# Keys and queries of a third head ahead of the second layer's norm, and one convolution ahead of the fourth head's projections

## The chip, the cores and the metric

The kernel runs on one NeuronCore of a Trainium2 chip. The metric is the device time of one execution in microseconds (us), given as the median of three runs of the kernel before.

## The reference

Two groups of tokens, 128 context tokens and 256 latent tokens, go through two layers with the same weights. Each layer norms and modulates its input `x`, projects it once to everything that three mixers need, projects their joined outputs back onto `x`, and then runs a squared-ReLU MLP.

```python
h = _rmsnorm(xs, norm_mix[d]) * (1.0 + ca) + sa
q, k, v, gb, gc, xin, u, vs = _project(h, w_in[d])
...
att = _diff_attention(q, k_all, v_all, lam, subln[d], lam_init)
conv = gb * _short_conv(gc * xin, conv_w[d], conv_b[d])
cmlp = _chunk_mlp(u, vs, w_s[d], b_s[d])
xs = xs + ga * (jnp.concatenate([att, conv, cmlp], axis=-1) @ w_out[d])
h = _rmsnorm(xs, norm_mlp[d]) * (1.0 + cm) + sm
xs = xs + gm * _mlp(h, w_up[d], w_down[d])
```

The attention has four heads; each takes the difference of two softmaxes. Context tokens attend to themselves, latent tokens to a cache and to themselves. All of it is in float32.

## The kernel before

**Precision and tiles.** Every long product is made of three matmuls in a faster 32-bit format: high part times high part (L220), high part of the weight times low part of the input (L221), low part of the weight times high part of the input (L222). `hh` and `hl` are the two parts of the input, 8 tiles of 128 features by 384 tokens. A weight chunk of 128x1024 arrives by DMA as `raw`; ScalarE (ACT) rounds it into `whi` (L201) and VectorE (DVE) makes `wlo` of the rest (L203).

**Order of the work.** The order on PE (TensorE), ACT, DVE and POOL (GpSimd) is written out by hand. The long products advance a clock by one tick per contraction step (three matmuls). All other work is cut into stages by Python generators, and a stage's number in the table `WAIT` says how many ticks go by before the next stage is issued. Ticks only set the order of the instructions on each engine; at run time an engine waits for what the next instruction of its list needs.

**The second layer's mixer.** While the last MLP tile of the first layer ends, `hh` and `hl` hold `x` times its feature scale, without the token's norm and without the shift. The keys and queries of the first `NPRE[d]` heads are projected from this form (tiles `pkq`, L634, 386 columns of which two carry the shift), and DVE multiplies the norm in when it moves them out of PSUM (`evict_all`, L512 and L514). Then `normed` (L355 to L378) writes the full normed input over `hh` and `hl`, a feature tile per stage: DVE makes `t` (L361), ACT writes `hh` (L369), DVE writes `hl` (L372). It can write a feature tile only when the last `pkq` product has read it, and `wait_normed` says at which tick it starts. PE goes on with the values (`nat`, `proj_tokens`, L448 to L450; two feature tiles to a weight chunk, three groups of tokens to a feature tile), which read each feature tile of the full norm, then with the later heads' keys and queries (`later_heads`), two convolutions (`conv`) and the chunk MLP.

**Attention.** Each head has three units `u` of 128 queries (`attention`, L720): scores `sc` (two PSUM tiles, L728 for the context unit, L731 and L732 for the others), their maxima on DVE (`nm`, L736), exponentials on ACT (`e`, L741), a scaling on DVE and ACT (L745 to L749), a transposition on PE (`pt`, L753), and after the third unit the product with the values (`po`). Units of a head are 8 ticks apart (`unit`), heads 24 (`head`), and the first starts `unit0` ticks after the values begin. The tiles `sc` and `pt` take turns in three PSUM buffers of the tag `misc`:

```python
def misc_tile(name="misc"):
    return ps.tile([P, 512], F32, tag="misc", name=name, bufs=3)
...
    for u in range(3):
        go(attention(h, u))
        yield wt["unit"]
```

Rotary positions (`rope_apply`) use a shuffle on DVE (L648) and three operations on POOL; `keys` and `queries` then make their parts on ACT (L666, L669, L682) and DVE (L670, L685).

Of the kernel before, what the change touches and what calls it, by code (L numbers as in the profile page):

```python
# [27 lines left out]
# heads of a layer whose products go ahead of the norm  # L28
NPRE = (3, 2)
# parts of the first modulation vector  # L30
PARTS = 4

# contraction steps between the stages of the work beside the long products, by layer
# [29 lines left out]
    "fh0": (14, 14),  # L63
# [9 lines left out]
    "wait_normed": (1, 12),  # L73
# [6 lines left out]
    "unit0": (24, 24),  # L80
    "head": (24, 24),
    "late": (0, 5),
# [4 lines left out]
# columns of the packed small operands: those of all layers that come first, then the rest  # L87
# [5 lines left out]
# order of the 128-column tiles of the input projection  # L93
Q0, K0, V0, GB0, GC0, XI0, U0, VS0 = 0, 512, 1024, 1536, 1792, 2048, 2304, 2560

# tokens, followed by one column for the shift of each group
# [4 lines left out]
def dit_kernel(ctx, tc, xT, cT, wmod, wmodT, wall, ck, cv, ws, lam, bs_in, small, rope, ident_in, yT, kT_out, v_out):  # L101
    nc = tc.nc
# [9 lines left out]
    # ---- constants and inputs  # L112
# [16 lines left out]
    # silu of the two conditioning vectors, as padded stationary columns  # L129
# [8 lines left out]
    # ---- the order of work: every engine runs in the order below. What is not part of the long  # L138
    # products is cut into stages; a stage names how many contraction steps of the long products
    # go by before the next one.  # L140
# [33 lines left out]
    def steps(gen, n, every):  # L174
        """n stages of a generator"""
        for i in range(n):
            next(gen, None)
            if i < n - 1:
                yield every

    # ---- weight streaming
# [8 lines left out]
    def refill(r=None):  # L190
        """the next chunk of the weights, in two parts"""
        i = state["chunk"]
        if i == wall.shape[0]:
            return
        state["chunk"] = i + 1
        if r is None:
            r = raw_chunk(wall[i])
        hi = wpool.tile([P, 1024], F32R, tag="whi", name="whi", bufs=4)
        lo = wpool.tile([P, 1024], F32R, tag="wlo", name="wlo", bufs=4)
        ready.append((hi, lo))  # L200
        nc.scalar.copy(hi, r)  # L201
        yield 2
        nc.vector.tensor_sub(lo, r, hi.bitcast(F32))  # L203
# [13 lines left out]
    def mm3(out, w, a, wsl, asl, first, last):  # L217
        """out += w.T @ a from the parts of both, w stationary"""
        (wh, wl), (ah, al) = w, a
        mm(out, wh[wsl], ah[asl], start=first, stop=False)  # L220
        mm(out, wh[wsl], al[asl], start=False, stop=False)  # L221
        mm(out, wl[wsl], ah[asl], start=False, stop=last)  # L222

    # ---- modulation vectors, features on partitions: modv[d][:, v, dt, group]
# [4 lines left out]
    def mod_done(d, v, base, dts=slice(0, KT)):  # L229
        """modv[d][:, v] = base + b_mod, and what scales the normed input"""  # L230

        def column(o):
            c = sm[:, d * S_LAYER + o + dts.start : d * S_LAYER + o + dts.stop]
            return c.unsqueeze(2).to_broadcast([P, dts.stop - dts.start, 2])

        nc.vector.tensor_add(modv[d][:, v, dts], base[:, dts], column(S_BMOD + v * KT))
        if v in (1, 4):
            nc.vector.scalar_tensor_tensor(
                (amix if v == 1 else amlp)[d][:, dts],
                modv[d][:, v, dts],  # L240
                1.0,
                column(S_NMIX if v == 1 else S_NMLP),
                ALU.add,
                ALU.mult,
            )

    def mod_products():
        """on the tensor engine: one feature tile of the contraction per step"""
        for i, (d, v) in enumerate(MOD_PE):
            pm = ps.tile([P, 256], F32, tag="mod", name="pm", bufs=1)  # L250
            tr = work.tile([P, KT, 32], F32, name="tr", tag="rtmp", bufs=1)
            # the first vector comes in parts of its features
            n = per = PARTS if i == 0 else 1
            width = 256 // n
            for f in range(n):
                own = slice(f * width, f * width + width)
                for q in range(KT // per):
                    w = ahead if (i, f, q) == (0, 0, 0) else raw_chunk(wmod[i, f * KT // per + q])
                    for k in range(per):
                        kt = q * per + k  # L260
                        for j in range(4):
                            mm(  # L262
                                pm[32 * j : 32 * j + 32, own],
                                sct[:, kt, :],
                                w[:, (4 * k + j) * width : (4 * k + j + 1) * width],
                                start=(kt == 0),
                                stop=(kt == KT - 1),
                            )
                    yield
                dts = slice(f * KT // n, (f + 1) * KT // n)  # L270
                nc.vector.transpose(tr[:, dts].rearrange("p a b -> p (a b)"), pm[:, own])
                mod_done(d, v, tr[:, :, 0:2], dts)
                yield
# [4 lines left out]
    # the two silu vectors along the free dimension, on every partition  # L278
# [4 lines left out]
    def spread_silu():  # L283
        """their high and low parts as rows, 32 features of each tile a row; then the sums of both parts"""
# [21 lines left out]
    def mod_sums():  # L306
        """on the vector engine: one group of one tile of the vector's features per step"""
        for i, (d, v) in enumerate(MOD_DVE):
            mr = work.tile([P, KT, 2], F32, name="mr", bufs=2)
            for dt in range(KT):  # L310
                w = raw_chunk(wmodT[i, dt])
# [12 lines left out]
    # ---- RMS statistics over the features (partitions)  # L324
# [13 lines left out]
    def rsqrt_refined(y, a, ms):  # L338
        """y ~ ms^-0.5 made exact by one Newton step"""
        nc.vector.tensor_mul(a, y, y)  # L340
        nc.vector.scalar_tensor_tensor(a, a, -0.5, ms, ALU.mult, ALU.mult)
        nc.vector.scalar_tensor_tensor(y, a, 1.5, y, ALU.add, ALU.mult)
# [12 lines left out]
    def normed(scale, shift, every):  # L355
        """the normed and modulated input, a feature tile per stage"""
# [23 lines left out]
    def scaled_high(dt, scale):  # L380
        """a feature tile without its tokens' norms, which products take on afterwards"""
# [24 lines left out]
    def finish_x(dt, pacc, gate, scale, last=False):  # L406
        """the residual stream's tile after a product, and what the next norm needs of it"""
# [12 lines left out]
    def proj_tiles(a, n=1, cols=T, name="acc", order=tuple(range(KT)), later=0, make=acc_tile):  # L420
        """128-column tiles of a weight, transposed: [column, token]"""
# [11 lines left out]
    def proj_tokens(a, width):  # L433
        """`width` columns of a weight, tokens on partitions: three tiles [token, column]"""
# [21 lines left out]
    def shift_products(raws, bias, t0, t1):  # L456
        """what the shift adds to the columns of the raw tiles: [column, tile, group]"""
# [17 lines left out]
    # padded conv input: 0 | prompt | 0 | sample | 0  # L475
# [8 lines left out]
    def lambdas(d):  # L484
# [10 lines left out]
        # -(e1 - e2 + li)  # L495
# [5 lines left out]
    for d in range(DEPTH):  # L501
# [5 lines left out]
        def evict(i):  # L507
            """a head's keys or queries but for the shift's part, which comes later"""
# [20 lines left out]
        # ------------------------------------------------ mixer  # L529
        # products with the tiles of two heads go ahead of the norm  # L530
# [85 lines left out]
        else:  # L616
# [16 lines left out]
            for i in (2, 3):  # L633
                pre.append(proj_tiles(a, 1, TE, "pkq", later=wt["later"]))  # L634
                evict_all(i)
# [17 lines left out]
        def keys(h):  # L653
            """positions, and the parts of the keys by component: the high ones on both halves, the low
            ones next to the queries' high ones"""
# [16 lines left out]
        def queries(h):  # L672
            """positions, and the parts of the sample's queries by component: high and low ones on the
            two halves, the high ones on the component's own"""
# [45 lines left out]
        def attention(h, u):  # L720
            """softmaxes of 128 queries of a head, combined and applied to the values"""
# [56 lines left out]
            # norm of the head's output, tokens on partitions  # L778
# [45 lines left out]
        def conv(ct):  # L824
            """short convolution, channels on partitions"""
# [54 lines left out]
        if d == 0:  # L880
            conv(0)
        later_heads()
        for ct in range(1 - d, 2):
            conv(ct)
# [6 lines left out]
        # output projection  # L891
# [7 lines left out]
        # ------------------------------------------------ MLP  # L899
        if d == 1:  # L900
            start(steps(sums, 2 * KT, wt["sums_up"]), 2)
        for f in range(2):
# [33 lines left out]
            def down(pt, w, c, cols):  # L936
                """half of the contraction of a tile"""
# [13 lines left out]
    # ---- the last tiles, a group of tokens after the other, and the final norm of each group  # L951
# [40 lines left out]
# the vectors (layer, which) in the order of their use, by the engine that makes them  # L992
# [6 lines left out]
def _tiles(w, cols):  # L999
    """[1024, cols of one 128-tile] -> [128, 8 * 128]"""  # L1000
# [5 lines left out]
def _pack(inp):  # L1006
# [6 lines left out]
    # [d, k, (v dt j c)] -> [v, kt, p, (j dt c)] and [v, dt, p, k]  # L1013
    # the first vector: [part, some kt, p, (kt j dt c)]
# [9 lines left out]
    for d in range(DEPTH):  # L1024
# [6 lines left out]
        if d == 0:  # L1031
            chunks += convs[0] + kq[n:] + convs[1]
        else:
            chunks += kq[n:] + convs[0] + convs[1]
# [32 lines left out]
    # axial rotary tables by shape: partition = (component, axis, half, frequency)  # L1067
# [34 lines left out]
```

## Time and profile before

| | us |
|---|---|
| median of three runs (918.04 to 920.19) | 919.28 |
| span of the profiled execution, from its first to its last instruction | 916.9 |
| median less that span (start and end around it) | 2.4 |
| PE busy in the span | 894.1 |
| DVE busy | 652.9 |
| ACT busy | 478.5 |

The page gives no time of its own for the profiled execution, only the span, so its own time is taken as the span and the 2.4 us around it. The second layer's mixer lies at 476 to 600 us of the span. A row of the timeline gives the start, the length, the engine, the line and what is written from what; matmuls overlap, so the distance of two starts is what one costs.

### The profile page before, as it was taken

How to read it: one execution, taken by the hardware profiler on the slowest of the kernel's cores; microseconds unless marked ns; L12 is line 12 of the kernel's file. 1: busy time of each engine (PE TensorE's matmuls, PEld its weight loads, DVE VectorE, ACT ScalarE, POOL GpSimd, SP SyncE). 2: the span in 40 equal slices, each digit the busy share in tenths (PEclk: the TensorE clock that was granted, in tenths of full speed). 3: DMA queues.
4: the chain of work that ended last, by engine and by line, in shares of the span. 5: the costliest groups of instructions: out<-in, count | busy, mean ns of one | idle time of the engine just before them, and what ended most of it. 6: DMA issues, size and time to landing. Idle time of an engine off the chain costs nothing.

```text
span 916.9 us, 14490 instructions
## 1 busy us (share of the span) xinstructions
PE 894.1 (98%) x5476; PEld 839.8 (92%) x5476; DVE 652.9 (71%) x1214; ACT 478.5 (52%) x938; POOL 81.3 (9%) x79
## 2 busy tenths in 40 slices
PE   5999999999999999999999999999999999999996
PEld 4766787999999999999998788999999999999996
DVE  4688886789888877879979877458886344555333
ACT  4557765446762226663336786534676223665331
POOL 0004320011000000000112340003000000000021
PEclk9999999999999999999999899999999999999998
DMA  9877566455656765566773323224465434333302
GB/s 346 298 274 252 192 209 226 165 182 161 209 188 226 227 214 180 183 198 226 221 234 101 125 76 95 91 93 138 163 221 169 137 117 136 115 133 121 115 1 69
DMA packets 48470, 156.55 MB, mean 171 GB/s; under 512 B 5392, under 2 KB 11024, under 8 KB 48400
## 3 DMA queue, kind: packets, MB, share of 16 engines
q1 hardware_dynamic: 48400, 155.63, 51.4%
q8 instruction: 43, 0.70, 0.3%
q14 instruction: 27, 0.22, 0.1%
HBM read 152.98 MB, written 2.62 MB: 170 GB/s over the span
## 4 chain that ended last, share of the span: by engine, by line
PE 91%; DVE 5%; DMA 1%; issue 1%; ACT 1%; POOL 1%; SPq 0%; DVEq 0%; ACTq 0%
PE pdn L220 10%; PE pdn L222 10%; PE pdn L221 10%; PE pup L221 9%; PE pup L220 9%; PE pup L222 9%; PE po L220 2%; PE po L221 2%; PE po L222 2%; PE pm L262 2%; PE pkq L220 2%; PE pkq L221 2%; PE pkq L222 1%; PE po L776 1%; PE nat L448 1%; PE sc L732 1%
## 5 line engine op out<-in xcount | busy, mean ns | idle before, releaser
L201 ACT CAST whi<-raw 128x1024 fp32r<-128x1024 f32 x182 | 190.0, 1050 | 293.3 <-PE pdn L221 150.9
L203 DVE TENSOR_TENSOR wlo<-raw,whi 128x1024 fp32r<-128x1024 f32 x182 | 224.6, 1240 | 64.9 <-ACT whi L201 64.8
L220 PE MATMUL pdn<-ah,whi 128*128 128x384 f32 (+2 forms) x528 | 174.7, 331 | 0.0
L221 PE MATMUL pdn<-al,whi 128*128 128x384 f32 (+2 forms) x528 | 174.6, 331 | 0.0
L222 PE MATMUL pdn<-ah,wlo 128*128 128x384 f32 (+2 forms) x528 | 174.6, 331 | 0.0
L220 PE MATMUL pup<-hh,whi 128*128 128x386 f32 x512 | 174.1, 340 | 0.0
L221 PE MATMUL pup<-hl,whi 128*128 128x386 f32 x512 | 173.6, 339 | 0.3
L222 PE MATMUL pup<-hh,wlo 128*128 128x386 f32 x512 | 172.8, 337 | 0.0
L314 DVE SCALAR_TENSOR_TENSOR junk<-raw,cb 128x1024 bf16<-128x1024 f32 x112 | 136.7, 1220 | 0.4
L221 PEld LDWEIGHTS pdn<-al,whi 128*128 128x128 f32 x528 | 99.2, 188 | 0.0
L220 PEld LDWEIGHTS pdn<-ah,whi 128*128 128x128 f32 x528 | 99.2, 188 | 0.0
L222 PEld LDWEIGHTS pdn<-ah,wlo 128*128 128x128 f32 x528 | 99.2, 188 | 0.0
L221 PEld LDWEIGHTS pup<-hl,whi 128*128 128x128 f32 x512 | 96.9, 189 | 1.1 <-DVE hl L387 0.9
L220 PEld LDWEIGHTS pup<-hh,whi 128*128 128x128 f32 x512 | 96.4, 188 | 0.3
L222 PEld LDWEIGHTS pup<-hh,wlo 128*128 128x128 f32 x512 | 96.5, 188 | 0.0
L336 POOL TENSOR_TENSOR sacc<-sacc,sq 128x384 f32<-128x384 f32 x23 | 29.4, 1279 | 675.6 <-ACT sq L329 533.7
L917 ACT ACTIVATE relu<-relu,ub 128x128 f32<-128x128 f32 (+1 forms) x128 | 51.1, 446 | 17.4 <-DVE relu L914 17.4
L398 DVE SCALAR_TENSOR_TENSOR x<-pdn,modv,x 128x128 f32<-128x128 f32 (+1 forms) x62 | 23.0, 413 | 43.9 <-PE pdn L222 43.9
L921 DVE TENSOR_TENSOR al<-relu,ah 128x384 fp32r<-128x384 f32 x64 | 35.6, 556 | 15.0 <-ACT ah L919 14.8
L220 PE MATMUL po<-y,whi 128*128 128x384 f32 x128 | 43.0, 336 | 0.0
L222 PE MATMUL po<-y,wlo 128*128 128x384 f32 x128 | 42.8, 334 | 0.0
L221 PE MATMUL po<-y,whi 128*128 128x384 f32 x128 | 42.8, 334 | 0.0
(198 smaller groups left out, 1414.1 us busy)
## 6 DMA issues: line engine op xcount, KB each, us to landing
raw<-in_wall_dram SPq DMA_DIRECT2D x182, 512.0 KB, 3.6
raw<-in_wmodT_dram SPq DMA_DIRECT2D x56, 512.0 KB, 4.3
raw<-in_wmod_dram SPq DMA_DIRECT2D x40, 512.0 KB, 5.7
raws<-in_wall_dram SPq DMA_DIRECT2D x6, 512.0 KB, 8.0
x<-in_xT_dram SPq DMA_DIRECT2D x8, 192.0 KB, 7.8
out_dram<-x SPq DMA_DIRECT2D x4, 256.0 KB, 2.6
mix<-in_cv_dram SPq DMA_DIRECT2D x2, 256.0 KB, 5.7
mix<-in_ws_dram SPq DMA_DIRECT2D x2, 256.0 KB, 6.0
```

The costliest lines, as they stand in the source:

```text
L201: nc.scalar.copy(hi, r)
L203: nc.vector.tensor_sub(lo, r, hi.bitcast(F32))
L220: mm(out, wh[wsl], ah[asl], start=first, stop=False)
L221: mm(out, wh[wsl], al[asl], start=False, stop=False)
L222: mm(out, wl[wsl], ah[asl], start=False, stop=last)
L262: mm(pm[32 * j : 32 * j + 32, own], sct[:, kt, :], w[:, (4 * k + j) * width : (4 * k + j + 1) * width], start=(kt == 0), stop=(kt == KT - 1),)
L314: nc.vector.scalar_tensor_tensor(junk, w, 1.0, cb[:, g], ALU.mult, ALU.mult, accum_out=mr[:, dt, g : g + 1])
L336: eng.tensor_add(stat["acc"], stat["acc"], sq)
L398: nc.vector.scalar_tensor_tensor(x[:, dt, a:b], pacc[:, a:b], gate[:, dt, g : g + 1], x[:, dt, a:b], ALU.mult, ALU.add)
L448: mm(o, ah, wh[:, cols], start=(kt == 0 and tt % n == 0), stop=False)
L917: nc.scalar.activation(r[:, s0:s1], r[:, s0:s1], AF.Relu, bias=ub[:, g : g + 1])
L921: nc.vector.tensor_sub(al[:, i], r, ah[:, i].bitcast(F32))
```

## The change

In the second layer the keys and queries of three heads, not two, are projected ahead of the norm; the norm starts 16 ticks later (`wait_normed` 28 for 12), so that it stands to the values as before. The first convolution comes ahead of the later head's keys and queries in both layers (it did so in the first layer already), and the weights are packed in that order. The third head's keys and queries are taken up 16 ticks after the second's, not 14 (`fh0`, which in the second layer had no use before). The first attention unit starts 17 ticks after the values begin, not 24 (`unit0`), and the last two heads have no further delay (`late`). The scratch space for DMA descriptors is made smaller. Comments are taken out, which shifts line numbers from L881 on.

```diff
-NPRE = (3, 2)
+NPRE = (3, 3)
...
-    "fh0": (14, 14),
+    "fh0": (14, 16),
...
-    "wait_normed": (1, 12),
+    "wait_normed": (1, 28),
...
-    "unit0": (24, 24),
+    "unit0": (24, 17),
...
-    "late": (0, 5),
+    "late": (0, 0),
...
-            for i in (2, 3):
+            for i in range(2, 2 * NPRE[d]):
...
-        if d == 0:
-            conv(0)
+        conv(0)
         later_heads()
-        for ct in range(1 - d, 2):
-            conv(ct)
+        conv(1)
...
-        if d == 0:
-            chunks += convs[0] + kq[n:] + convs[1]
-        else:
-            chunks += kq[n:] + convs[0] + convs[1]
+        chunks += convs[0] + kq[n:] + convs[1]
...
-    nc = bacc.Bacc("TRN2", target_bir_lowering=False, num_devices=1)
+    nc = bacc.Bacc("TRN2", target_bir_lowering=False, num_devices=1, dynamic_dma_scratch_size=4096)
```

How this moves instructions is shown at three places, before and after. The number behind a name tells tiles of one name apart; the names in brackets are the engines that a row waits for.

**PE, values of the second layer, the first unit's scores (L728).** Before, they stand behind the sixth of eight feature tiles (`whi_5045` holds the fifth and sixth, `whi_5113` the last two):

```order
L448 MATMUL nat_5084<-whi_5045,hh_97 128x512
L449 MATMUL nat_5084<-wlo_5046,hh_97 128x512
L450 MATMUL nat_5084<-whi_5045,hl_98 128x512
L728 MATMUL sc_5250<-mix_4917 128x128
L728 MATMUL sc_5251<-mix_4917 128x128
L448 MATMUL nat_5082<-whi_5113,hh_97 128x512 [waits Activation_49]
L449 MATMUL nat_5082<-wlo_5114,hh_97 128x512
```

With the change:

```order
L448 MATMUL nat_5149<-whi_5112,hh_97 128x512 [waits Activation_49]
L449 MATMUL nat_5149<-wlo_5113,hh_97 128x512
L450 MATMUL nat_5149<-whi_5112,hl_98 128x512 [waits DVE_49]
L728 MATMUL sc_5280<-mix_4917 128x128
L728 MATMUL sc_5281<-mix_4917 128x128
L448 MATMUL nat_5150<-whi_5112,hh_97 128x512 [waits Activation_49]
L449 MATMUL nat_5150<-wlo_5113,hh_97 128x512
L450 MATMUL nat_5150<-whi_5112,hl_98 128x512 [waits DVE_49]
```

The two score products now stand behind the first token group of the fifth feature tile (`whi_5112` holds the fifth and sixth), five groups earlier.

**PE, the second unit's scores (L731 and L732).** Before, they stand behind the last feature tile of the values, ahead of the third head's keys `pk`:

```order
L448 MATMUL nat_5084<-whi_5113,hh_97 128x512
L449 MATMUL nat_5084<-wlo_5114,hh_97 128x512
L450 MATMUL nat_5084<-whi_5113,hl_98 128x512
L731 MATMUL sc_5294<-kh_5135,qs_5195 128x384
L732 MATMUL sc_5294<-kl_5136,qs_5195 128x384
L731 MATMUL sc_5295<-kh_5135,qs_5195 128x384 [waits Activation_49]
L732 MATMUL sc_5295<-kl_5136,qs_5195 128x384
L220 MATMUL pk_5310<-hh_97,whi_5141 128x384 [waits PE_49]
L221 MATMUL pk_5310<-hl_98,whi_5141 128x384
L222 MATMUL pk_5310<-hh_97,wlo_5142 128x384
```

With the change:

```order
L448 MATMUL nat_5149<-whi_5180,hh_97 128x512 [waits Activation_49]
L449 MATMUL nat_5149<-wlo_5181,hh_97 128x512
L450 MATMUL nat_5149<-whi_5180,hl_98 128x512 [waits DVE_49]
L731 MATMUL sc_5340<-kh_5202,qs_5262 128x384 [waits DVE_49]
L732 MATMUL sc_5340<-kl_5203,qs_5262 128x384
L731 MATMUL sc_5341<-kh_5202,qs_5262 128x384 [waits Activation_49]
L732 MATMUL sc_5341<-kl_5203,qs_5262 128x384
L448 MATMUL nat_5150<-whi_5180,hh_97 128x512
L449 MATMUL nat_5150<-wlo_5181,hh_97 128x512
L450 MATMUL nat_5150<-whi_5180,hl_98 128x512
```

They now stand behind the first token group of the seventh feature tile (`whi_5180` holds the last two), so five groups of the values are queued behind them. The wait of the second product (`sc_5341`) for ACT is there before and after: its PSUM buffer is the one in which the first unit's first scores were.

**DVE, end of the norm (`hl`, L372) and first unit.** Before:

```order
L685 TENSOR_TENSOR qs_5195<-mix_4917,qs_5195 64x256 x2
L372 SCALAR_TENSOR_TENSOR hl_98<-t_5200,modv1_92,hh_97 128x128 [waits Activation_49]
L372 SCALAR_TENSOR_TENSOR hl_98<-t_5200,modv1_92,hh_97 128x256 [waits Activation_49]
L203 TENSOR_TENSOR wlo_5208<-raw_5205,whi_5207 128x1024 [waits DMAHW5_49,PE_49]
L648 STREAM_SHUFFLE rt_5235<-mix_4917 128x256 [waits Pool_49]
L670 TENSOR_TENSOR kl_5229<-mix_4917,kh_5228 64x384 [waits DMAHW4_49,Activation_49]
L670 TENSOR_TENSOR kl_5229<-mix_4917,kh_5228 64x384 [waits Activation_49]
L736 TENSOR_REDUCE nm_5262<-sc_5250 128x1 [waits PE_49]
L736 TENSOR_REDUCE nm_5262<-sc_5251 128x1 [waits PE_49]
L203 TENSOR_TENSOR wlo_5257<-raw_5254,whi_5256 128x1024 [waits DMAHW7_49,Activation_49]
L745 RECIPROCAL s_5270<-s_5270 128x2 [waits Activation_49]
L746 TENSOR_SCALAR s_5270<-s_5270,neg_lam_104 128x1 [waits DVE_49]
```

With the change:

```order
L685 TENSOR_TENSOR qs_5262<-mix_4917,qs_5262 64x256 x2
L372 SCALAR_TENSOR_TENSOR hl_98<-t_5267,modv1_92,hh_97 128x128 [waits Activation_49]
L372 SCALAR_TENSOR_TENSOR hl_98<-t_5267,modv1_92,hh_97 128x256 [waits Activation_49]
L203 TENSOR_TENSOR wlo_5275<-raw_5272,whi_5274 128x1024 [waits DMAHW0_49,PE_49]
L736 TENSOR_REDUCE nm_5296<-sc_5280 128x1 [waits PE_49]
L736 TENSOR_REDUCE nm_5296<-sc_5281 128x1 [waits PE_49]
L648 STREAM_SHUFFLE rt_5313<-mix_4917 128x256 [waits Pool_49]
L670 TENSOR_TENSOR kl_5303<-mix_4917,kh_5302 64x384 [waits DMAHW4_49,Activation_49]
L670 TENSOR_TENSOR kl_5303<-mix_4917,kh_5302 64x384 [waits Activation_49]
L745 RECIPROCAL s_5307<-s_5307 128x2 [waits Activation_49]
L746 TENSOR_SCALAR s_5307<-s_5307,neg_lam_104 128x1 [waits DVE_49]
L749 SCALAR_TENSOR_TENSOR e_5306<-e_5306,s_5307 128x128 [waits Activation_49]
```

The maxima `nm` of the first unit now come ahead of the second head's shuffle and `kl`, and its reciprocal ahead of the next `wlo`. The 44 rows on DVE from the first `t` of the norm (L361) to the `wlo` shown here are the same rows in the same order before and after, and they stand behind the move of the last but one `pkq` tile out of PSUM in both.

## Rows read from the trace of the kernel before

**Rows 1.** the page: its span, and section 1, busy us and share of the span

```profile
span 916.9 us, 14490 instructions
...
PE 894.1 (98%) x5476; PEld 839.8 (92%) x5476; DVE 652.9 (71%) x1214; ACT 478.5 (52%) x938; POOL 81.3 (9%) x79
```

**Rows 2.** windows, 504 to 514 us: length, busy us by engine, PEclk, DMA share, GB/s

```profile
504.00:506.00 2.00, 0.21 (x1) 0.21 (x2) 2.00 (x5) 1.01 (x4) 0.93 (x1) 0.77 0.32 59
506.00:508.00 2.00, 2.00 (x5) 1.61 (x6) 2.00 (x6) 2.00 (x6) 1.34 (x2) 0.50 0.51 207
...
510.00:512.00 2.00, 2.00 (x5) 1.59 (x6) 1.97 (x4) 1.38 (x2) 0.00 (x0) 0.53 0.01 4
512.00:514.00 2.00, 2.00 (x10) 1.64 (x9) 1.94 (x6) 0.00 (x0) 1.38 (x2) 1.00 0.40 115
```

**Rows 3.** the waits of PE, 440 to 640 us: in total, times, longest

```profile
PE nat L450 <- DVE hl L372: 2.8, 1, 2.8
```

**Rows 4.** timeline of PE, 487 to 523 us: start, us, engine, line, operation

```profile
487.50 0.34 PE L220 MATMUL pkq<-hh,whi 128*128 128x386 f32 x1
...
491.73 0.40 PE L448 MATMUL nat<-whi,hh 128*128 128x512 f32 x1
...
492.43 0.39 PE L448 MATMUL nat<-whi,hh 128*128 128x512 f32 x1
...
505.79 0.80 PE L450 MATMUL nat<-whi,hl 128*128 128x512 f32 x1 [2.83 <-DVE hl L372]
506.38 0.63 PE L448 MATMUL nat<-whi,hh 128*128 128x512 f32 x1
...
507.66 0.63 PE L448 MATMUL nat<-whi,hh 128*128 128x512 f32 x1
...
509.07 0.80 PE L728 MATMUL sc<-mix 64*128 64x128 f32 x4
...
515.02 0.34 PE L731 MATMUL sc<-kh,qs 128*128 128x384 f32 x1
...
516.40 0.44 PE L220 MATMUL pk<-hh,whi 128*128 128x384 f32 x1
...
522.21 0.44 PE L220 MATMUL pq<-hh,whi 128*128 128x384 f32 x1
```

**Rows 5.** timeline of DVE, 487 to 518 us

```profile
487.70 0.16 DVE L622 COPY bias<-pkq 128x2 f32<-128x2 f32 x1 [0.98 <-PE pkq L222]
...
505.39 0.73 DVE L372 SCALAR_TENSOR_TENSOR hl<-t,modv,hh 128x128 fp32r<-128x128 f32 x2
...
509.32 0.85 DVE L685 TENSOR_TENSOR qs<-mix,qs 64x256 fp32r<-64x256 f32 x2
...
510.87 1.22 DVE L203 TENSOR_TENSOR wlo<-raw,whi 128x1024 fp32r<-128x1024 f32 x1
...
512.35 1.56 DVE L670 TENSOR_TENSOR kl<-mix,kh 64x384 fp32r<-64x384 f32 x2
513.94 0.49 DVE L736 TENSOR_REDUCE nm<-sc 128x1 f32<-128x128 f32 x2
...
515.60 0.16 DVE L745 RECIPROCAL s<-s 128x2 f32<-128x2 f32 x1
...
516.95 0.35 DVE L749 SCALAR_TENSOR_TENSOR e<-e,s 128x128 f32<-128x128 f32 x1
517.22 1.01 DVE L736 TENSOR_REDUCE nm<-sc 128x1 f32<-128x384 f32 x2
```

**Rows 6.** timeline of ACT, 514 to 519 us

```profile
514.27 0.37 ACT L741 ACTIVATE e<-sc,nm 128x128 f32<-128x128 f32 x1 [2.86 <-DVE nm L736]
...
516.10 0.40 ACT L747 ACTIVATE e<-e,s 128x128 f32<-128x128 f32 x1 [0.31 <-DVE s L746]
...
518.78 0.60 ACT L741 ACTIVATE e<-sc,nm 128x384 f32<-128x384 f32 x1
```

**Rows 7.** the waits of PE weight loads, 60 to 200 us (first layer)

```profile
PEld sc L731 <- ACT e L741: 0.5, 1, 0.5
```

## Prediction

> **What bounds the kernel now.** I read the page first: PE is busy for 98% of the 916.9 us [rows 1], so time can only come from the places where PE waits, or be lost where it begins to. Next I asked for PE's waits from the end of the first layer to the start of the second MLP, the stretch that the change touches: there is one, 2.8 us in the values, for the low part `hl` of a feature tile [rows 3]. It shows again in PE's timeline, idle up to 505.79 [rows 4]. Then the windows around it: the granted clock falls to 0.50 while PE stands (0.77 is the mean of the window in which it falls), and is back at 1.00 only from 512 us [rows 2]. A group of three value matmuls costs 492.43 - 491.73 = 0.70 us at the upper level (2.4 GHz) and 507.66 - 506.38 = 1.28 at the lower (1.2 GHz) [rows 4]. Last the timelines of DVE and ACT: DVE works without a gap from 487.70, when it moves the last but one `pkq` tile out of PSUM, until the `hl` at 505.39 that frees PE and beyond [rows 5]. So PE waits for the amount of work on DVE, not for one slow operation. The median of the runs is 2.4 us above the profiled span; I make the sum as a difference against that execution and put it on the median of 919.28.
>
> **The change, on the old time axis.** A `pkq` tile is 491.73 - 487.50 = 4.23 us [rows 4]. Two more of them come ahead of the values and two fewer behind, so everything from the norm on is 8.46 us later and this is given back after the convolution; the 386 columns instead of 384 are 0.04 us for both tiles, nothing. I leave the 8.46 out of all times below.
>
> *The norm.* DVE's 44 rows from the first `t` to the `wlo` behind the last `hl` are unchanged, and before them stands the same move of a `pkq` tile, which waits for PE (0.98 us idle in front of it [rows 5]), now for the fifth tile instead of the third. So DVE starts the row of work at the same distance to the values and hands over `hl` at the same 505.79. The two tiles that DVE now also moves out fall into the time in which it idles; without that cover they would cost their own length, as the 0.98 us show at most. The wait stays.
>
> *First unit's scores.* They move ahead of that wait. At 509.07 they took up to 0.8 us at the lower level [rows 4]; now I take half, 0.4, at the upper. PE thus arrives 0.4 later and waits 2.4 instead of 2.83; what is saved is the 0.8 that no longer lies behind 505.79.
>
> *Second unit's scores.* PE resumes at 505.79, still at the lower level: the rest of a group, 0.59, then three groups of 1.28, and it stands at the second unit at 510.2. Their input `qs` is done at 509.32 + 0.85 = 510.17 [rows 5], just in time. The first product pair ends at about 511.2 (an estimate: 0.69 for half a unit at the upper level, from 515.02 to 516.40, stretched as the groups are, is 1.26; I take 1.0, since part of it is loading weights). The second pair needs the PSUM buffer of the first unit's scores, hence its exponential. On DVE the maxima come behind the `wlo` that ends at 510.87 + 1.22 = 512.09; before, the exponential began 514.27 - 513.94 = 0.33 after them, and takes 0.37 [rows 5, 6]. So it ends at 512.8, and PE goes on at 512.9: a new wait of 1.7 us. Behind it on PE stand five groups of the values, which everything later waits for. That this buffer can hold PE up is seen in the first layer, where a score's weight load stood 0.5 us for the same exponential [rows 7].
>
> *From there to the third unit.* At the upper level: the pair 0.69, three groups 2.1, and PE asks for the first unit's transposition at 515.7. DVE has it ready at: maxima until 512.58, shuffle and `kl` until about 514.5 (`kl` 1.56), then reciprocal to scaled result 516.95 + 0.35 - 515.60 = 1.70 less the `qs` 0.87 that stood in between (0.85 and its gap), plus 0.4 for waiting on ACT's 0.40: 515.8 [rows 5, 6]. That is even, 0.1 of waiting. Two groups and a tick (0.53) later, at 517.9, PE stands at the third unit, whose first buffer needs the second unit's exponential: DVE does a `wlo` 1.22 and a bias, its maxima (half of 1.01) end at 518.0, the exponential (0.60) at 518.7 [rows 5, 6]. Another wait of 0.9, and the third unit ends at 518.8 + 1.4 = 520.2.
>
> *The sum.* Before, PE ends the third unit at 522.21, having done eight ticks of the third head's keys; with the change one tick of the convolution. The seven ticks are 7 x 0.53 = 3.7 us [rows 4]: 520.2 + 3.7 = 523.9, against 522.21: **1.7 us lost**. The clock's recovery at 512 is taken as before. If no wait came after 512.9, PE would end at 519.2 and 0.7 be lost; if the second unit's wait did not form either, PE would end that unit at 510.2 + 2.0 = 512.2 and the third, with five groups, a transposition, a tick and a unit behind it (3.5 + 0.1 + 0.5 + 1.4), at 517.7; with the 3.7 that is 521.4, and 0.8 is gained. Those are the near ends.
>
> *The rest.* The convolution ahead of the fourth head, the heads' new distances and `late` move matmuls among matmuls where PE has no wait up to 640 us [rows 3]; the cover is that DVE and ACT keep up with units 8 ticks apart, which they did there. Were it gone, the next to be late would be a unit's transposition, by less than a unit's 1.4 us each. The third head's cached keys and its key output go on SP's queue at nearly the same distance behind the values as before, with weight loads around them; those wait on no transfer in this stretch. The DMA scratch serves descriptors that POOL writes, and the page shows none: nothing. At the mixer's end the fourth head's result comes four ticks (2.1 us) nearer to its use in the output projection; ten ticks (5.3 us) are left from its transposition to there, for one ACT and one DVE operation.
>
> **The rivals.**
>
> *The clock stays low (slower).* Three waits of 2.4, 1.7 and 0.9 us now lie within 16 us. If the clock is still at the lower level when PE resumes at 512.9 and stays there, the 6.2 us of work to the end of the third unit (0.7, five groups 3.5, 0.1, a tick 0.5, a unit 1.4) take 6.2 x 1.28/0.70 = 11.3, and the end is 524.2, 4.0 later than above: 5.7 in all, 925.0. For it: one wait alone brought the clock down and PE then worked some 6 us before it rose [rows 2, 4]. Against it: PE is busy again from 512.9 nearly throughout. It decides at whether the row at 513 (521 on the new axis) is at 0.50. [...]
>
> *The new waits don't form (no change).* If DVE comes to the first unit's maxima about 2 us earlier, the end is 521.4: 918.5. For it: all of DVE's lengths are from one execution, with POOL running beside it, and that overlap may fall otherwise. Against it: POOL's own order is unchanged.
>
> *The old wait goes (faster).* If the same accident gives `hl` 2.4 us earlier, PE keeps its clock and saves 2.4 and about half of the 6 us at the lower level: 5.4, 913.9. Against it stand the 44 unchanged rows; this would also be the case in which the later norm start does more than I can see.
>
> **How the numbers follow.** A measurement of this kernel tells about 0.2% (1.84 us) from no change, so "same" is 917.44 to 921.12. My forecast, 919.28 + 1.7 = **921.0**, has 0.45, with a range of its own from 919.5 to 922.4; it lies at the upper edge of "same" and gives it 0.26, slower 0.19. The lasting low clock has 0.20, all slower. No new waits has 0.22: same 0.20, faster 0.02. The old wait gone has 0.13, all faster. Together: faster 0.15, same 0.46, slower 0.39. The range goes from 917.4 (it leaves out the old wait gone) to 924.4 (it leaves out the worst of the low clock).
>
> **What would show it.** In the changed profile: PE's wait in the values still there, for `hl`, at about 514 us and about 2.4 long; a second for ACT's L741 at the second unit's L731, near 521, and a small third near 527; granted clock 0.50 between. The forecast is wrong if the first wait is gone or under 1 us, if PE passes the second unit without a wait, or if PE waits in the convolutions or the output projection.

## The result, and the profile after

| | before | after |
|---|---|---|
| median of seven runs each, us | 918.13 (916.00 to 920.19) | 921.20 (920.97 to 924.48) |
| ratio, 95% interval | | 1.0043 (1.0030 to 1.0056) |
| span of the profiled execution, us | 916.9 | 920.3 |
| time of the profiled execution, us | | 922.09 |

The change makes the kernel 0.43% slower, 3.1 us by the medians and 3.4 us by the two profiled spans. Start and end around a span take 1.8 us here (922.09 - 920.3), not the 2.4 that the prediction took from a median and a span of different executions.

The page of the changed kernel, its span and its section 1, against [rows 1]:

```profile
span 920.3 us, 14503 instructions
...
PE 895.0 (97%) x5476; PEld 839.9 (91%) x5476; DVE 653.8 (71%) x1220; ACT 478.5 (52%) x939; POOL 79.9 (9%) x79
```

PE is busy for 0.9 us longer and the span is 3.4 longer: the rest is idle time of PE. PE's waits from 440 to 660 us of the changed kernel (in total, times, longest), against [rows 3]:

```profile
PE sc L731 <- ACT e L741: 2.5, 2, 2.2
PE nat L450 <- DVE hl L372: 2.2, 1, 2.2
```

The old wait for `hl` is still there; a new one stands at the second score product. The windows of the changed kernel, 512 to 524 us (length, busy us by engine, PEclk, DMA share, GB/s), against [rows 2]:

```profile
512.00:514.00 2.00, 0.26 (x2) 0.00 (x0) 2.00 (x3) 0.99 (x3) 1.59 (x1) 1.00 0.13 37
514.00:516.00 2.00, 1.55 (x4) 1.28 (x5) 2.00 (x7) 2.00 (x5) 0.74 (x1) 0.70 0.86 260
516.00:518.00 2.00, 2.00 (x6) 1.56 (x5) 1.99 (x4) 1.91 (x5) 1.53 (x2) 0.50 0.01 2
518.00:520.00 2.00, 1.25 (x4) 0.46 (x3) 1.94 (x5) 0.00 (x0) 0.00 (x0) 0.95 0.00 0
520.00:522.00 2.00, 0.50 (x1) 0.21 (x1) 1.97 (x7) 0.99 (x5) 0.41 (x1) 0.90 0.19 23
522.00:524.00 2.00, 2.00 (x5) 1.44 (x5) 1.41 (x4) 1.34 (x4) 1.47 (x2) 0.50 0.60 240
```

PEclk, the granted clock, falls to 0.50 twice, once behind each wait. PE is nearly empty in 512 to 514 and again in 520 to 522, and DVE is full until 522 (its column stays at 1.94 or more). The timeline of PE of the changed kernel, against [rows 4]:

```profile
514.45 0.52 PE L450 MATMUL nat<-whi,hl 128*128 128x512 f32 x1 [2.19 <-DVE hl L372]
...
518.44 0.44 PE L731 MATMUL sc<-kh,qs 128*128 128x384 f32 x1
521.50 0.61 PE L731 MATMUL sc<-kh,qs 128*128 128x384 f32 x1 [2.25 <-ACT e L741]
...
527.95 0.34 PE L731 MATMUL sc<-kh,qs 128*128 128x384 f32 x1
...
529.33 0.44 PE L220 MATMUL pgc<-hh,whi 128*128 128x384 f32 x1
```

The second unit is at 518.44, its second product at 521.50, the third unit at 527.95, its end at 529.33. DVE of the changed kernel, against [rows 5]:

```profile
496.35 0.16 DVE L622 COPY bias<-pkq 128x2 f32<-128x2 f32 x1 [2.11 <-PE pkq L222]
...
514.05 0.74 DVE L372 SCALAR_TENSOR_TENSOR hl<-t,modv,hh 128x128 fp32r<-128x128 f32 x2
...
517.96 0.87 DVE L685 TENSOR_TENSOR qs<-mix,qs 64x256 fp32r<-64x256 f32 x2
...
519.53 1.22 DVE L203 TENSOR_TENSOR wlo<-raw,whi 128x1024 fp32r<-128x1024 f32 x1
520.67 0.48 DVE L736 TENSOR_REDUCE nm<-sc 128x1 f32<-128x128 f32 x2
...
526.01 1.01 DVE L736 TENSOR_REDUCE nm<-sc 128x1 f32<-128x384 f32 x2
```

From the `pkq` move to the `hl` it is 17.70 us, before 17.69 [rows 5]: the row is the same, 8.65 us later. The first unit's maxima `nm` come at 520.67, directly behind a `wlo`. ACT of the changed kernel, against [rows 6]:

```profile
520.99 0.37 ACT L741 ACTIVATE e<-sc,nm 128x128 f32<-128x128 f32 x1 [3.05 <-DVE nm L736]
...
526.59 0.58 ACT L741 ACTIVATE e<-sc,nm 128x384 f32<-128x384 f32 x1 [1.03 <-DVE nm L736]
```

So the chain of the new wait is: DVE's row, maxima at 520.67, exponential at 520.99, PE at 521.50.

**Where the 3.4 us lie.** I added up the distances of starts on PE, from the first `pkq` matmul to the first of the output projection: 126.72 us before, 129.69 after. By the end of the third unit the loss is 2.2 (6.94 us later than before, of which nine ticks more, two `pkq` tiles less seven ticks of keys, are 4.76); the L732 rows there have grown by 2.57, and these hold the 2.25 us wait. From there to the output projection another 0.8 is lost, in rows that show no wait but one of 0.2: later context scores 0.4, long products 0.3, values of 256 columns 0.2, less 0.1 elsewhere. The remaining 0.4 lies ahead of this stretch and behind it, 0.2 each; what lies behind is the last head's transposition `pot`, which now comes after the first output products and no longer ahead of them.

### The profile page after: what moved, and what is told of

Read it like the earlier page. It is cut to its first block, busy times and chain, and to the rows that moved or that the text cites. A ratio compares the mean times of both kernels' runs of the same rounds, so it can differ in the third digit from the quotient of the medians.

```text
span 920.3 us, 14503 instructions
## 1 busy us (share of the span) xinstructions
PE 895.0 (97%) x5476; PEld 839.9 (91%) x5476; DVE 653.8 (71%) x1220; ACT 478.5 (52%) x939; POOL 79.9 (9%) x79
## 4 chain that ended last, share of the span: by engine, by line
PE 90%; DVE 5%; issue 1%; DMA 1%; ACT 1%; POOL 1%; SPq 0%; DVEq 0%; ACTq 0%
PE pdn L222 10%; PE pdn L220 10%; PE pdn L221 10%; PE pup L221 9%; PE pup L220 9%; PE pup L222 9%; PE po L222 2%; PE po L220 2%; PE po L221 2%; PE pm L262 2%; PE pkq L220 2%; PE pkq L221 2%; PE pkq L222 2%; PE po L776 1%; PE sc L732 1%; PE nat L448 1%
```

## The experiments

**My theory:** the whole loss is in one number, `unit0` 17, which brings the first attention units to PE before DVE can serve them; three heads ahead of the norm, the order of the convolution and the scratch size cost nothing. The rivals: the projections' new order, the shared PSUM buffer, or the scratch.

**e1: the change with the units at their old distance.**

```diff
-    "unit0": (24, 17),
+    "unit0": (24, 24),
```

> The changed kernel with one number put back: the first attention unit starts 24 ticks after the values begin, as before, not 17. Theory (the loss is the earlier attention, whose scores stand among the values while DVE is still at the norm): the second unit's wait of 2.2 us for the exponential is gone, one wait of 2.2 to 2.8 us for hl stays, and the time is that of the kernel before within 1 us (917 to 919). Rival (three heads ahead of the norm, or the convolution ahead of the fourth head, cost the time themselves): it stays at 920 to 921.5.

Measured: 918.46 us (11 runs; before 918.72), ratio 0.9996 (0.9987 to 1.0004). PE's waits, 440 to 660 us:

```profile
PE nat L450 <- DVE hl L372: 2.8, 1, 2.8
PE sc L731 <- ACT e L741: 0.7, 1, 0.7
```

The loss is gone, the 2.8 us are there as in [rows 3]. Everything else in the change is neutral together, within the 0.13% of the interval.

**e2: only that number, in the kernel before.**

```diff
-    "unit0": (24, 24),
+    "unit0": (24, 17),
```

> The kernel before with only the first unit's start moved from 24 to 17 ticks; two heads ahead of the norm and the old order of the convolutions. Theory (earlier attention alone makes the loss): PE waits for L741 at the second unit's scores as in the changed kernel, about 2.2 us, and the time is about 3 us above before (920.5 to 922). Rival (the third head and the convolution): no second wait, 917 to 919.

Measured: 924.58 us, ratio 1.0064 (1.0050 to 1.0078): one and a half times the loss of the whole change, and more than I expected. PE's waits, 440 to 660 us:

```profile
PE nat L450 <- DVE hl L372: 2.5, 2, 2.2
PE sc L731 <- ACT e L741: 2.2, 1, 2.2
PE pt L753 <- DVE e L749: 1.5, 2, 1.2
PE po L776 <- ACT ats L764: 1.1, 1, 1.1
PE sc L731 <- DVE qs L685: 0.9, 1, 0.9
```

The same two waits as in the changed kernel, and three more. The number alone makes the loss. The rest of the change seems to give some 2 to 3 us back where attention starts early (1.0064 against 1.0043; the two intervals touch). Which part of the rest does this, the third head or the convolution's place, was not tried.

**e3: the changed kernel, with another PSUM buffer for the first unit's first scores,** the one that the second unit's second product waited for.

```diff
-        sc = [misc_tile("sc") for c in range(2)]
+        sc = [misc_tile("sc") if c or u or not d else ps.tile([P, 256], F32, tag="mod", name="sc", bufs=1) for c in range(2)]
```

> The changed kernel, but the first scores of each head's first unit in the second layer get a PSUM bank of their own (the one that the modulation products used in the first layer), so the second unit need not wait for the first unit's exponential. If the row of work on DVE is what binds: the wait moves to the first unit's transposition (L753), 2 us there, and the time falls by 0.5 to 1 us, to 920 to 920.7. Rival (the shared buffer alone is the cause): the wait is gone, the second low stretch of the clock with it, and the time falls by 3 us or more, to 918 or less.

Measured: 921.34 us, ratio 1.0029 (1.0019 to 1.0040). The largest of PE's waits, 440 to 660 us:

```profile
PE nat L450 <- DVE hl L372: 2.2, 1, 2.2
PE pt L753 <- DVE e L749: 1.8, 1, 1.8
PE sc L731 <- ACT e L741: 1.3, 2, 0.7
```

and its window of the longest new wait:

```profile
522.00:524.00 2.00, 0.16 (x3) 0.13 (x2) 1.30 (x5) 1.34 (x3) 0.99 (x2) 1.00 0.53 213
```

The wait moved to the transposition, as the theory had it: the buffer was the place of the wait, DVE's row its cause. The time was a miss: no fall is shown, as the median is not below the changed kernel's 921.20 and the intervals overlap. The second low stretch of the clock is gone (PEclk 1.00 from 520 us on), and still the stretch from the first `pkq` to the output projection takes 129.34 us against 129.69. So the wait at the buffer and the low clock behind it cost no more than 0.4 us beyond what the wait at the transposition costs; what binds is DVE's row.

**e4: the norm freed instead, in the kernel before.** The heads' rotary work and the units come later, so that DVE reaches the norm's end earlier.

```diff
-    "heads": (4, 1),
-    "unit0": (24, 24),
-    "head": (24, 24),
+    "heads": (4, 8),
+    "unit0": (24, 28),
+    "head": (24, 22),
```

> The kernel before, with the first heads' rotary work in the second layer begun 8 ticks after the values begin, not 1 (so that one shuffle, one kl and most of POOL's work leave DVE's row ahead of the sixth hl), the first unit at 28 ticks and heads 22 ticks apart. Theory (PE waits in the values because of the amount of work on DVE): hl is ready at about 502 us of the old axis, before PE asks for it at 502.9; no wait, the granted clock stays at 1.00, and 5 to 6 us are saved (912 to 914). Rival (the norm's own work, or ACT, sets the wait): the wait stays at 1.5 us or more and the time within 2 us of before.

Measured: 926.86 us, ratio 1.0095 (1.0081 to 1.0109). PE's waits, 440 to 660 us, and the first unit's maxima on DVE:

```profile
PE sc L731 <- ACT e L741: 3.2, 1, 3.2
PE pot L797 <- DVE o L791: 2.7, 1, 2.7
PE pt L753 <- ACT atp L762: 1.4, 1, 1.4
...
PE nat L450 <- DVE hl L372: 0.2, 1, 0.2
```

```profile
513.73 0.49 DVE L736 TENSOR_REDUCE nm<-sc 128x1 f32<-128x128 f32 x2
```

The wait came out, the time missed by 13 us. The wait for `hl` fell from 2.8 to 0.2, so it does come from the amount of work that DVE does ahead of it. But the maxima come no earlier: 40.59 us after the first `pkq` (513.73 - 473.14), before 39.78 (513.94 [rows 5] - 474.16). PE got there earlier and waited there, and later heads, now closer together, waited as well.

**e5 and e8: the scratch size alone,** put into the kernel before and taken out of the changed one.

```diff
-    nc = bacc.Bacc("TRN2", target_bir_lowering=False, num_devices=1)
+    nc = bacc.Bacc("TRN2", target_bir_lowering=False, num_devices=1, dynamic_dma_scratch_size=4096)
```

> The kernel before with only the smaller scratch for DMA descriptors. Every theory but one: no difference (within 0.2% of before), PE's waits unchanged. Rival (the scratch holds back DMA issues): slower by over 0.2%, with weights landing later.

> The changed kernel with the scratch of the DMA descriptors back at its old size, and nothing else. Theory (the size bears on nothing, the units that stand too early are the whole loss): 920.5 to 922.0 us as the changed kernel, 1.003 to 1.005 of the kernel before; the wait for the projection's split values 2.0 to 2.9 us and the one of the second score product 2.0 to 2.9 us as in the changed kernel. Rival (the smaller scratch makes part of the loss, as its run on the kernel before at 1.002 may say): 918 to 919.5 us.

Measured: e5 919.43 us, ratio 1.0020 (1.0009 to 1.0032); e8 921.53 us, ratio 1.0043 (1.0027 to 1.0059). Taking the smaller scratch out of the changed kernel changes nothing that these runs can tell: the same ratio, nearly the same waits (2.2 us for `hl`, 2.0 at the second score product), 129.72 us from the first `pkq` to the output projection against 129.69. So I take it as no part of the loss.

Why the kernel before came out 0.2% longer with the smaller scratch stays open. None of its ten runs showed the mean clock of 0.997 that 9 of the 23 runs of the kernel before beside it had (see the last section). Its trace tells more than its time, since the clock fell elsewhere in this execution. In the second layer the wait for `hl` is as long as ever, but the clock stays at 1.00 behind it, and a wait at the second score product appears in the old order of the units:

```profile
507.65 0.49 PE L450 MATMUL nat<-whi,hl 128*128 128x512 f32 x1 [2.82 <-DVE hl L372]
516.64 0.44 PE L731 MATMUL sc<-kh,qs 128*128 128x384 f32 x1 [1.57 <-ACT e L741]
```

```profile
508.00:510.00 2.00, 2.00 (x12) 1.33 (x10) 2.00 (x4) 2.00 (x5) 1.47 (x2) 1.00 0.48 195
```

From the first `pkq` PE reaches the second unit 2.5 us sooner than in the kernel before (38.36 us against 40.86), but its second product only 0.9 sooner (40.63 against 41.50), and the output projection 0.9 sooner (125.86 against 126.72). The first unit's maxima come at the same distance, 39.79 and 39.78. So nearly two thirds of what the full clock saves on PE is waited away at DVE's row, and this wait needs no early unit. Its first `pkq` comes 1.85 us later than in the kernel before (476.01 against 474.16). Most of that was lost in the first layer, where the clock fell behind a wait of 0.64 us that the kernel before has too, with the clock left at 1.00:

```profile
84.00:86.00 2.00, 2.00 (x7) 2.00 (x7) 1.31 (x3) 2.00 (x6) 0.00 (x0) 0.50 0.62 182
```

**e7 and e6: the changed kernel with later units, and with a freed norm too.** e7:

```diff
-    "unit0": (24, 17),
-    "head": (24, 24),
+    "unit0": (24, 32),
+    "head": (24, 21),
```

e6:

```diff
-    "heads": (4, 1),
-    "unit0": (24, 17),
-    "head": (24, 24),
+    "heads": (4, 8),
+    "unit0": (24, 36),
+    "head": (24, 20),
```

> The changed kernel with the rotary work where it was (1 tick), the first unit at 32 ticks and heads 21 apart. Theory: the wait for hl stays as it is in the kernel before (2.8 us, clock down once), no wait at the scores: 917 to 919, as with 24 ticks or up to 1 us less. Rival (later attention alone is what frees the norm): the wait for hl shrinks too and the time falls below 915.

> The changed kernel with the first heads' rotary work begun 8 ticks after the values begin, the first unit at 36 ticks and heads 20 ticks apart, so that neither the rotary work nor the attention stands in DVE's row ahead of the sixth hl, and PE has the rest of the values and half of the first convolution's first product to do before it needs the first unit. Theory (one row of work on DVE sets both waits, so both have to move behind the norm): no wait over 0.5 us in the values or at the scores, granted clock 1.00 throughout the mixer, 911.5 to 914. Rival (the wait only moves to a later unit or to the output projection, since DVE has no room anywhere): 916 or more, with a wait of over 2 us at a later unit or for the fourth head's y.

Measured: e7 919.39 us, ratio 1.0019 (1.0004 to 1.0033), with the wait for `hl` of 2.8 and one of 0.8 for ACT. e6 923.98 us, ratio 1.0073 (1.0058 to 1.0088), with 0.2 us for `hl`, and then, of PE's waits from 440 to 660 us:

```profile
PE sc L728 <- ACT e L741: 5.1, 2, 2.7
PE pxi L220 <- ACT mix L877: 1.3, 1, 1.3
```

The longer of the two waits for `e` in e6 ends by ACT's order, in which a `kh` and other jobs stand ahead of the exponential; ahead of the other, at 537.55 us, ACT itself waited for DVE's maxima:

```profile
536.83 0.58 ACT L741 ACTIVATE e<-sc,nm 128x384 f32<-128x384 f32 x1 [1.50 <-DVE nm L736]
```

Units later than 24, with heads 21 apart, gain nothing, and heads 20 ticks apart are too dense for DVE and ACT. The rival of e6 was right: what is taken from one wait comes back at the next.

**e9: a looser order of the same kind.** The second head's rotary work comes behind the first unit's maxima (`fh3` 14 for 5), and the norm is freed. The expectation names another move than the edit makes: `fh3` ticks stand behind each head's queries, so the second head's work goes from 13 to 29 ticks after the values begin and the third's from 41 to 50.

```diff
-    "fh0": (14, 16),
-    "fh3": (5, 5),
-    "heads": (4, 1),
-    "unit0": (24, 17),
-    "head": (24, 24),
+    "fh0": (14, 0),
+    "fh3": (5, 14),
+    "heads": (4, 8),
+    "unit0": (24, 26),
+    "head": (24, 23),
```

> The changed kernel with the third head's rotary work moved from axis 8 to 14 (the pair of the second head stays with its projection), the unit's start from 17 to 26, its heads 23 apart. Theory (VectorE's row up to the first unit's maxima is what counts; with one head's rotary work behind them the norm and the maxima both come early): the wait for the split values under 0.5 us, those at the score products 1 us in sum, the clock above 0.9 from 512 us on, 912.5 to 915 us. Rival (VectorE has no room, the work put back comes due at the second unit instead): waits of 2 us or more at a later score product or transposition, 917 us or more.

Measured: 923.44 us, ratio 1.0058 (1.0043 to 1.0073); `hl` 0.2 us, but 3.4 at a later L728 and 2.1 in sum at L731, each for the exponential. The rival again.

**e10 and e12: the later rotary work alone,** in the changed kernel with the units at 24, and in the kernel before, whose second layer has no use for `fh0`. e10:

```diff
-    "fh0": (14, 16),
-    "fh3": (5, 5),
-    "unit0": (24, 17),
+    "fh0": (14, 6),
+    "fh3": (5, 14),
+    "unit0": (24, 24),
```

e12:

```diff
-    "fh0": (14, 14),
-    "fh3": (5, 5),
+    "fh0": (14, 6),
+    "fh3": (5, 14),
```

> The changed kernel with the same rotary work moved later, but the norm left at its place, and the units at 24. Theory: the wait for the split values stays near 2.8 us, as it stands behind VectorE's norm and not behind rotary work; no other wait above 1 us; 917 to 919 us, as with the units at 24 alone. Rival (the rotary work is what the split values wait for): the wait falls below 1.5 us and the time to 914 to 916 us.

> The kernel before, with the second head's rotary work moved from axis 5 to 14 as in the run that measured 916.4 us. Theory (that run's 1.5 us come from this work being no longer between the first unit's maxima and their exponential, and not from the three heads): the wait for the split values stays 2 to 3 us, the kernel gains as much here, 915.5 to 917.5 us. Rival (three heads ahead of the norm are needed for it): no gain, 918 to 920 us, with a wait of 1 us or more at a score product or a transposition.

Measured: e10 916.41 us, ratio 0.9982 (0.9972 to 0.9992), faster than both kernels and below what its theory allowed; e12 917.28 us, ratio 0.9991 (0.9982 to 1.0001), not told from no change. The one wait of PE in e10, 440 to 660 us:

```profile
PE nat L450 <- DVE hl L372: 2.3, 1, 2.3
```

The wait in the values stays. Of the changed kernel with its units at 24 (e1), the wait of 0.7 at L731 is gone. In e12 the first unit's maxima are earlier than in [rows 5] by 3.5 us:

```profile
510.46 0.47 DVE L736 TENSOR_REDUCE nm<-sc 128x1 f32<-128x128 f32 x2
```

So the traces point to what DVE does between the end of the norm and the first maxima: from the first `pkq` to the second MLP's first product e12 takes 158.74 us, before 160.11. e12's median lies within its theory, though its ratio alone doesn't show a gain; and that three heads ahead help in e10 is not shown, as the two intervals overlap.

**e11: e10 with the norm three steps freer.**

```diff
-    "fh0": (14, 6),
-    "heads": (4, 1),
+    "fh0": (14, 3),
+    "heads": (4, 4),
```

> The run of 916.4 us with the heads' work three steps later, so that the norm's split values come ahead of one more piece of it. Theory (the second score product there has 1.8 us between its exponential at 518.3 and its start at 520.2, so that this much of the wait of 2.3 us can go without a new one): the wait for the split values 0.6 to 1.6 us, other waits under 0.5 us in sum, 914.5 to 916 us. Rival (VectorE's row to the first unit's maxima is the bound): what the first wait loses comes back at the second score product or later, 916 to 918 us.

Measured: 919.36 us, ratio 1.0019 (1.0004 to 1.0034). PE's waits, 440 to 660 us:

```profile
PE sc L731 <- ACT e L741: 3.1, 1, 3.1
PE nat L450 <- DVE hl L372: 0.6, 1, 0.6
```

DVE ends the second unit's maxima at 521.67 + 1.02 = 522.69, but ACT makes its exponential at 527.04. The row of the maxima, and ACT's timeline behind it:

```profile
521.67 1.02 DVE L736 TENSOR_REDUCE nm<-sc 128x1 f32<-128x384 f32 x2
...
522.39 1.05 ACT L666 CAST kh<-mix 64x384 fp32r<-64x384 f32 x2 [0.32 <-POOL mix L651]
523.46 1.05 ACT L201 CAST whi<-raw 128x1024 fp32r<-128x1024 f32 x1
524.42 1.55 ACT L877 COPY mix<-nat 128x512 f32<-128x512 f32 x3
525.98 1.03 ACT L669 CAST kh<-mix 64x384 fp32r<-64x384 f32 x2
527.04 0.58 ACT L741 ACTIVATE e<-sc,nm 128x384 f32<-128x384 f32 x1
```

The `hl` wait fell as expected; in its place a longer one came, and now ACT's order makes it: one job is under way when the maxima end, and three more stand ahead of their exponential. The time was a miss by 3.4 us: the slack of 1.8 us that I had read lay between the first unit's exponential and the second unit only.

## Why the prediction was right, and where it was not

The sign, the places of the two large waits and the time (921.0 forecast, 921.20 measured) came out; the small third wait did not. The closeness of the time was partly luck: I put a loss of 1.7 on a median of 919.28. The loss is 3.1 to 3.4, and the median of the kernel before, over more runs, is 918.13. The two errors cancel.

- **The axis and the norm.** Right. All is 8.46 us later, and 0.2 from ahead of the stretch; the wait for `hl` ends at 514.45, which is 505.79 [rows 4] and 8.66. It is 2.2 long where I had 2.4, as PE came to it 0.6 later, not 0.4.
- **The second unit's wait.** Its end was forecast at 512.9, on the new axis 521.56; it was 521.50. It is 2.25 long, not 1.7, as PE came earlier (518.44, forecast 518.86): the clock was not yet down all through the window from 514 (0.70) and was back at 0.95 in the window from 518. The length of a wait that ends by another engine's row is not what it costs; its end is, and that was right. e1 and e2 show that the early units make the loss, e3 that the row of DVE and not the buffer alone holds the wait. That the wait as such is new was my reading of one execution: with the clock at 1.00 the kernel before has it too, 1.57 us (e5).
- **The step that failed: "The clock's recovery at 512 is taken as before."** It rose sooner than that, and then, behind the second wait, it fell again to 0.50 in the window from 522. So the way from the second product to the third unit took 527.95 - 521.50 = 6.45 us where I had 5.0 (my own terms for it add up to 4.8: PE would have asked at 517.7, not 517.9, and the near end without a third wait is 519.1, not 519.2). For the same reason **the third wait did not form**: the second unit's exponential ends at 526.59 + 0.58 = 527.17 (forecast 518.7, or 527.36), and PE came after it. Clock and wait stand in for each other: the third unit ended at 529.33, forecast 528.86, so the failure is worth 0.5 us.
- **"The rest" at nothing.** Another 0.8 us behind the third unit, with one wait of 0.2 in it, and 0.4 ahead of the mixer's stretch and behind it. I had no term for either.
- **The rivals.** The lasting low clock was half right: it came down twice, but not for good (0.90 in the window from 520, 0.50 in the next). The page "TensorE: Matmul & The Clock Gate" of the Trainium skill, section "HAM oscillation — how this bites in real kernels", tells of a kernel in which each DMA wait of about 3 to 5 us throttles the clock again, so that every next burst starts cold. Here the measurement decides: shorter waits had the clock at 0.50 behind them (2.83 us before, 2.19 and 2.25 in the changed kernel), and some did not (1.84 us in e3, 2.82 in e5). The other two rivals fell: the maxima came at 520.67, just as the sum had them, and the wait for `hl` stayed.

## What to carry to other kernels

Where an in-order engine's queue is full without a gap, moving its consumer's work earlier buys nothing: the consumer arrives sooner and waits longer, and each new wait may also cost it its clock. A faster consumer gains little there either: with the clock up throughout the mixer (e5) the stretch was 0.9 us shorter. Before moving work ahead, ask at what time the serving engine's row reaches it, and whether the row has become shorter; in e4 the maxima came no earlier than before. What gained here, 0.2% (e10), was to take work out of the row between one dependent step and the next, in a place where no consumer was near, and the next bound (e11) was already another engine.

## What was unexpected of the hardware

The same kernel runs at several mean clocks. Of 81 runs of the kernel before beside these experiments, 20 had a mean granted clock of 0.997 with a median of 916.58 us (916.03 to 917.67), 59 had 0.993 to 0.995 (917.25 to 920.43), and two 0.990 (920.54 and 921.39). The profiled execution of before is one of those at 0.993, with the fall of [rows 2]. A run at 0.997 was never profiled, so that the clock does not fall behind its `hl` wait is my guess; that this can happen is shown by e5, whose program differs only in the scratch size. All seven runs of the changed kernel had 0.990 to 0.993.

Nor does the length of a wait alone tell whether the clock falls. Behind 2.83 us it fell in the kernel before, behind 2.82 us in e5 it did not, and in the first layer the same 0.64 us went the other way around in the same two executions. The 1.84 us wait in e3 ended at 523.87 and left it at 1.00; in e9 PE stood 1.68 us up to 526.02, and the windows behind that read:

```profile
526.00:528.00 2.00, 1.98 (x6) 1.25 (x7) 1.01 (x3) 1.94 (x5) 1.14 (x2) 0.93 0.11 43
528.00:530.00 2.00, 2.00 (x8) 2.00 (x7) 1.43 (x2) 2.00 (x5) 0.00 (x0) 0.50 0.00 0
```

So a median of three or seven runs depends on how many of each kind it holds, at the extremes by more than the 0.2% below which the prediction saw no difference, and a comparison of two such kernels needs many runs.
